# A gated one-hot made by ScalarE from an absolute difference and a relu, in a one-core decoder layer

## The chip, the cores and the metric

The kernel runs on one core of a Trainium2 chip. The metric is the device time of one execution in microseconds (us). TensorE (PE) multiplies matrices into PSUM, VectorE (DVE) and ScalarE (ACT) work element by element, GpSimd (POOL) here only issues gathers, and SyncE (SP) issues the other transfers. Each engine works through its own list of instructions in order and waits for others by semaphores.

## What is computed

One layer of a decoder trunk for a prompt of 1024 tokens (8 tiles of 128) and 8 single-token samples. After the mixers (attention, spatial gating, a recurrent block) comes a layer of product-key experts. Cut to what matters:

```python
s = einsum('nhpe,hpke->nhpk', q, sub_keys)           # 8 heads, two key sets of 128
v1, i1 = top_k(s[:, :, 0], 16); v2, i2 = top_k(s[:, :, 1], 16)
sv, ci = top_k(all sums of v1 and v2, 16)             # 16 experts a head
e_idx = i1[...] * 128 + i2[...]                       # one of 16384 experts
g = softmax(sv)
act = gelu(einsum('nd,nkd->nk', x, u_tab[e_idx]))     # 128 experts a token
out = einsum('nk,nkd->nd', g * act, v_tab[e_idx])
```

Each token has 128 chosen experts, each with a first index i1, a second index i2 and a gate g, all in float32.

## The kernel before

The expert layer is done in two ways. Four tiles of tokens (0, 2, 6, 7) and the sample are **gathered**: for each of 128 slots GpSimd fetches the 128 rows of the table that the tile's tokens chose (an indirect DMA, line 916, five buffers named grow), VectorE multiplies and sums them against the tokens (line 924, table u) or adds them, scaled, to acc (lines 931 and 933, table v). That is 520 fetches from each table, in the order tile 0, 2, 6, 7, sample, u before v in each tile.

The four other tiles (1, 3, 4, 5) are **dense**: all 16384 experts are applied. For this a gate table is built, for each token a matrix of 128 by 128 with the gate at (i2, i1) and zero elsewhere. `select(t)` brings i1, i2 and g of a tile with tokens along the free side into `tr`. `gate_table(t)` walks through the tile in 8 steps of 16 tokens. For 4 tokens at a time VectorE makes one-hot rows of i1 and of i2 by comparing a row of 0..127 (`iof`) with the index (line 815, tile `oh12`); ScalarE scales the one-hot of i1 by the gate into `o1` (line 822, three buffers); TensorE multiplies the two one-hots (line 823, into the one bank psG), which sums over the 128 slots; ScalarE copies psG into two tiles `st` (line 825, two buffers in all), and SyncE writes these to DRAM (`g_d`). `dense()` then computes scores of all experts (line 1022), gelu, times the gate table (line 1027), splits into two parts for exact products (lines 991 and 992), and products with table v (line 1038) that stay in PSUM (psK) or are added to acc by VectorE (psO, line 1047), in 32 groups of 4 blocks of 128 experts.

The order of the program text is: four groups of tiles are projected and mixed (`project`, `mix_and_route`), the steps of `select` and `gate_table` of a dense tile are pumped into the attention and the routing of the next group, then `dense()`, then the gathers. A scheduler of the language orders each engine's list from this text by its own estimate of when things are ready, with earlier text first; the gathers, last in the text, fill gaps. So the row operations of lines 924, 931 and 933 stand spread over VectorE's whole list, from the second group on, and the list is fixed when the kernel is built. "The front" below is all up to the first split of `dense()` (line 992, x0l).

Of the kernel before, what the change touches and what calls it, by code (L numbers as in the profile page):

```python
# [10 lines left out]
F32 = mybir.dt.float32  # L11
# [49 lines left out]
def kernel(ctx: ExitStack, tc: tile.TileContext, I, O):  # L61
# [41 lines left out]
    class Early:  # L103
# [2 lines left out]

        def a2(self, name):
            self.n += 1
            shape, tag = (([P, P // 2, TB], "st"), ([P, 2, OHB, P], "oh12"))[self.n % 2]
            x = fr.tile(shape, F32, tag=tag, name=name, bufs=2)  # L110
            return x.rearrange("p a b -> p (a b)")[:, :512] if tag == "st" else x.rearrange("p a b c -> p (a b c)")[:, :512]
    X = Early()

    def a4(name):
# [656 lines left out]
    def select(t):  # L771
        if t == NT:

            tv[t] = (se.tile([P, 16, 16], F32, tag="tkv", name="tkv", bufs=3), se.tile([P, 16, 16], U32, tag="tki", name="tki", bufs=3))
            v1, x1 = (q[:, 0, :] for q in tv[t])
            sr = R.a2("sr")[:, :P]
            S.dma_start(sr, s_d.rearrange("b (s k) -> (b s) k", k=P))
            top16(sr, P, v1, x1, "tkw", P)
            S.dma_start(sv_d, v1)
            S.dma_start(sx_d, x1)  # L780
            v, x = (q[:64, 2:4, :] for q in tv[t])
            S.dma_start(v, sv_d.rearrange("(q two) k -> q two k", two=2))
            S.dma_start(x, sx_d.rearrange("(q two) k -> q two k", two=2))
            r, nh = 64, 1
        else:
            r, nh = P, 8
            v, x = tv[t]
        tv.pop(t)
        i1, i2, gt = (se.tile([P, 8, 16], F32, tag=nm, name=nm, bufs=1)[:r, :nh] for nm in ("d_i1", "d_i2", "d_g"))
        yield from select_experts(v, x, r, nh, i1, i2, gt)  # L790
        if t in h2_d:
            e = se.tile([P, 8, 16], I32, tag="d_q4", name="d_e", bufs=1)[:r, :nh]
            V.scalar_tensor_tensor(e, i1, float(P), i2, op0=ALU.mult, op1=ALU.add)
            for d, src in ((e_d[t], e), (w_d[t], gt)):
                S.dma_start(dram_ap(d, 0, [[16 * nh, r], [1, 16 * nh]]), src.rearrange("p h k -> p (h k)"))
            return
        ps = R.ps("psi")
        tr[t] = fr.tile([P, 3, P], F32, tag="tr", name="tr", bufs=2)
        for q, src in enumerate((i1, i2, gt)):
            T.transpose(ps[:, q * P:(q + 1) * P], src.rearrange("p h k -> p (h k)"), ident)  # L800
        A.copy(tr[t], ps[:, :3 * P].rearrange("p (q n) -> p q n", q=3))

    def gate_ps(name):
        return mm.tile([P, 512], F32, tag="pg", name=name, bufs=BANKS["g"])
# [1 line left out]
    def gate_table(t):  # L806
# [3 lines left out]
        for b in range(P // TB):  # L810
            sts = [fr.tile([P, P // 2, TB], F32, tag="st", name="st", bufs=2) for _ in range(2)]
            for n0 in range(0, TB, 4):
                if n0 % OHB == 0:
                    oh = fr.tile([P, 2, OHB, P], F32, tag="oh12", name="oh12", bufs=2)
                    V.tensor_tensor(oh, iof[:, None, None, :].to_broadcast([P, 2, OHB, P]),  # L815
                                    tt[:, 0:2, b * TB + n0:b * TB + n0 + OHB, None].to_broadcast([P, 2, OHB, P]),
                                    op=ALU.is_equal)
                ps = gate_ps("psG")
                for q in range(4):
                    n = b * TB + n0 + q  # L820
                    o1 = fr.tile([P, P], F32, tag="o1", name="o1", bufs=3)
                    A.activation(o1, oh[:, 0, n0 % OHB + q, :], AF.Copy, scale=tt[:, 2, n:n + 1])  # L822
                    T.matmul(ps[:, q * P:(q + 1) * P], oh[:, 1, n0 % OHB + q, :], o1, start=True, stop=True)  # L823
                for st, pv in zip(sts, ps.rearrange("p (n two c) -> two p c n", n=4, two=2)):
                    A.copy(st[:, :, n0:n0 + 4], pv)  # L825
            hg = P // GST // 2
# [376 lines left out]
```

## Time and profile before

| | |
|---|---|
| median of 3 runs | 3299.31 us (3297.56 to 3300.51) |
| profiled execution | 3299.12 us, span 3297.3 us |
| PE busy | 2775.9 us, 84% of the span |
| DVE busy | 2543.4 us, 77% |
| ACT busy | 1213.0 us, 37% |
| POOL busy | 1412.7 us, 43% |
| transfers | 952.64 MB, mean 289 GB/s |

Busy shares are means over the whole span, and the program has parts with different limits: read a share by the stretch. A matmul's busy time is modelled and overlaps its neighbours. The idle time of an engine tells what ended it, which is not always what the program waits for last.

### The profile page before, as it was taken

To read this page: it belongs to the slowest core of one execution; us is meant where nothing else is said; L and a number is where in the kernel's file an instruction comes from. 1 tells how busy PE (TensorE), PEld (TensorE's weight loads), DVE (VectorE), ACT (ScalarE), POOL (GpSimd) and SP (SyncE) were. 2 spreads that over 40 slices of the span, in tenths; PEclk is the share of its full clock that TensorE was granted. 3 is DMA by queue.
4 is the path that set the end of the run, shared out by engine and by line. 5 is a ranking of instruction groups with operands and counts; after the bars stand their busy time and mean duration, and the time that the engine had idled before them with its cause. 6 is when DMAs were issued, how large, how long until landed. Compare 5 with 4: busy or idle time off the path is not lost.

```text
span 3297.3 us, 35948 instructions
## 1 busy us (share of the span) xinstructions
PE 2775.9 (84%) x11152; PEld 1877.4 (57%) x11152; DVE 2543.4 (77%) x5342; ACT 1213.0 (37%) x2718; POOL 1412.7 (43%) x1046
## 2 busy tenths in 40 slices
PE   6889877888898799768699989988998989989980
PEld 2334435443365346544477877766777777767760
DVE  1432776788777797777998898788988888889895
ACT  3454336553476337654432222221322222222210
POOL 0000033454234322334146666465656646666564
PEclk8989988989899899878899999999999999999995
DMA  7555487988778876888789999899999999999986
GB/s 250 179 191 198 142 287 227 311 317 297 238 224 287 314 252 195 266 281 284 239 297 349 352 321 334 322 341 335 337 331 338 343 332 357 330 344 346 342 299 226
DMA packets 340719, 952.64 MB, mean 289 GB/s; under 512 B 35600, under 2 KB 118087, under 8 KB 338479
## 3 DMA queue, kind: packets, MB, share of 16 engines
q0 software_dynamic: 149760, 545.33, 47.0%
q1 hardware_dynamic: 190766, 405.02, 35.1%
q8 instruction: 88, 1.44, 0.2%
q14 instruction: 105, 0.85, 0.1%
HBM read 894.07 MB, written 60.88 MB: 290 GB/s over the span
## 4 chain that ended last, share of the span: by engine, by line
PE 26%; DMA 23%; issue 21%; POOL 16%; DVE 10%; ACT 4%; SPq 0%; POOLq 0%; DVEq 0%; ACTq 0%
POOL grow L916 16%; PE psz L249 10%; DMA grow<-in_peer_v,ge 9%; DMA g_d<-st 5%; PE psG L823 4%; PE pst L174 2%; PE pso L637 2%; PE lg L620 2%; DMA w<-in_w_in 1%; DVE grow L924 1%; PE psa L206 1%; DVE acc L933 1%; DMA grow<-in_peer_u,ge 1%; DMA w<-in_wq 1%; PE psS L1022 1%
## 5 line engine op out<-in xcount | busy, mean ns | idle before, releaser
L916 POOL DMA_INDIRECT grow<-in_peer_u,ge x520 | 699.2, 1345 | 1146.8 <-DVE grow L924 466.5
L916 POOL DMA_INDIRECT grow<-in_peer_v,ge x520 | 712.9, 1371 | 717.1 <-DVE acc L933 420.9
L933 DVE SCALAR_TENSOR_TENSOR acc<-grow,dot,acc 128x1024 f32<-128x1024 f32 x515 | 659.8, 1281 | 121.8 <-DMA grow<-in_peer_v,ge 115.0
L249 PE MATMUL psz<-w,hT 128*128 128x512 f32 x1408 | 699.3, 629 | 61.7 <-DMA w<-in_w_in 22.4
L924 DVE SCALAR_TENSOR_TENSOR grow<-grow,gx 128x1024 f32<-128x1024 f32 x520 | 626.1, 1219 | 152.9 <-DMA grow<-in_peer_u,ge 120.0
L249 PEld LDWEIGHTS psz<-w,hT 128*128 128x128 f32 x1408 | 257.6, 200 | 325.8 <-issue 228.3
L1038 PE MATMUL psO<-vh,ah 128*128 128x512 f32 x512 | 223.6, 437 | 139.3 <-DVE acc L1047 138.8
L991 ACT CAST vh<-v 128x1024 fp32r<-128x1024 f32 x128 | 125.2, 1048 | 495.1 <-PE psO L1038 493.2
L823 PEld LDWEIGHTS psG<-o,oh 128*128 128x128 f32 x1024 | 162.5, 220 | 168.3 <-ACT st L825 106.7
L823 PE MATMUL psG<-o,oh 128*128 128x128 f32 x1024 | 195.0, 323 | 74.9 <-ACT st L825 70.0
L991 ACT CAST ah<-a 128x512 fp32r<-128x512 f32 x128 | 79.7, 622 | 424.1 <-DVE a L1027 424.1
L815 DVE TENSOR_TENSOR oh<-iof,tr 128x1024 f32<-128x1024 f32 x128 | 156.4, 1224 | 94.8 <-PE psG L823 92.8
L1038 PE MATMUL psO<-vl,ah 128*128 128x512 f32 x512 | 217.5, 425 | 0.0
L1038 PE MATMUL psO<-vh,al 128*128 128x512 f32 x512 | 215.5, 421 | 0.0
L991 ACT CAST uh<-u 128x1024 fp32r<-128x1024 f32 x128 | 135.0, 1055 | 218.4 <-PE psS L1022 218.0
L1038 PEld LDWEIGHTS psO<-vh,ah 128*128 128x128 f32 x512 | 107.7, 210 | 178.0 <-DVE acc L1047 154.2
L822 ACT ACTIVATE o<-oh,tr 128x128 f32<-128x128 f32 x512 | 185.0, 400 | 50.9 <-PE psG L823 46.5
L1038 PE MATMUL psK<-vh,ah 128*128 128x512 f32 x512 | 200.0, 391 | 2.1 <-ACT ah L991 2.1
L1038 PE MATMUL psK<-vh,al 128*128 128x512 f32 x512 | 200.2, 391 | 0.2 <-DVE al L992 0.2
L1038 PE MATMUL psK<-vl,ah 128*128 128x512 f32 x512 | 199.9, 390 | 0.0
L992 DVE TENSOR_TENSOR ul<-u,uh 128x1024 fp32r<-128x1024 f32 x128 | 156.0, 1219 | 1.4 <-ACT uh L991 1.4
L992 DVE TENSOR_TENSOR vl<-v,vh 128x1024 fp32r<-128x1024 f32 x128 | 150.5, 1219 | 0.5 <-ACT vh L991 0.4
(370 smaller groups left out, 5009.1 us busy)
## 6 DMA issues: line engine op xcount, KB each, us to landing
u<-in_peer_uT SPq DMA_DIRECT2D x128, 512.0 KB
v<-in_peer_v SPq DMA_DIRECT2D x128, 512.0 KB
w<-in_w_in SPq DMA_DIRECT2D x80, 512.0 KB
w<-in_wq SPq DMA_DIRECT2D x64, 512.0 KB
g_d<-st SPq DMA_DIRECT2D x64, 512.0 KB
gc<-g_d SPq DMA_DIRECT2D x16, 2048.0 KB
w<-in_w_ada SPq DMA_DIRECT2D x48, 512.0 KB
w<-in_w_out SPq DMA_DIRECT2D x32, 512.0 KB
```

What stands on the lines that cost most here:

```text
L174: T.transpose(pv[:, c, :r], src[:, (c0 + c) * P:(c0 + c + 1) * P], ident[:r, :r])
L249: T.matmul(ps, xT[:, c, :], w(c), start=(c == 0), stop=(c == 7))
L620: T.matmul(l[:, :k1 - k0], qT[t][64 * hh:64 * hh + 64, hp, :], kT[64 * hh:64 * hh + 64, k0:k1], start=True, stop=True)
L815: V.tensor_tensor(oh, iof[:, None, None, :].to_broadcast([P, 2, OHB, P]), tt[:, 0:2, b * TB + n0:b * TB + n0 + OHB, None].to_broadcast([P, ...
L822: A.activation(o1, oh[:, 0, n0 % OHB + q, :], AF.Copy, scale=tt[:, 2, n:n + 1])
L823: T.matmul(ps[:, q * P:(q + 1) * P], oh[:, 1, n0 % OHB + q, :], o1, start=True, stop=True)
L916: G.indirect_dma_start(out=rt, out_offset=None, in_=tab, in_offset=bass.IndirectOffsetOnAxis(ap=idx, axis=0))
L924: V.scalar_tensor_tensor(rt, rt, 1.0, x, op0=ALU.mult, op1=ALU.mult, accum_out=w[:, k:k + 1])
L933: V.scalar_tensor_tensor(acc, rt, w[:, k:k + 1], acc, op0=ALU.mult, op1=ALU.add)
L991: A.copy(hi, x)
L992: eng.tensor_tensor(lo, x, hi, op=ALU.subtract)
L1038: T.matmul(ps, aa[x][:, t * P:(t + 1) * P], vv[y][:, hf * 512:(hf + 1) * 512], start=(k == 0 and (first or o not in keep)), stop=(k == 3 * ...
```

## The change

The one-hot of i1 with its gate is no longer a comparison on VectorE followed by a scaling on ScalarE. ScalarE makes it in two passes from the row 0..127: first |i1 - c| with the index as the bias column, then relu(g - g|i1 - c|), with the gate as the bias column and the negated gate as the scale column. Where c is the index this is g, elsewhere the argument is zero or below and the result zero. VectorE's comparison makes the one-hot of i2 alone. `tr` has a fourth part for the negated gates, and the one-hot tile is half as large with three buffers in place of two; the early sample attention, which borrows these tiles, alternates over the new ones.

```diff
 def a2(self, name):   # Early
-            shape, tag = (([P, P // 2, TB], "st"), ([P, 2, OHB, P], "oh12"))[self.n % 2]
-            x = fr.tile(shape, F32, tag=tag, name=name, bufs=2)
+            shape, tag = (([P, P // 2, TB], "st"), ([P, OHB, P], "oh2"))[self.n % 2]
+            x = fr.tile(shape, F32, tag=tag, name=name, bufs=2 if tag == "st" else 3)
...
-        tr[t] = fr.tile([P, 3, P], F32, tag="tr", name="tr", bufs=2)
+        tr[t] = fr.tile([P, 4, P], F32, tag="tr", name="tr", bufs=2)
...
-        A.copy(tr[t], ps[:, :3 * P].rearrange("p (q n) -> p q n", q=3))
+        A.copy(tr[t][:, 0:3, :], ps[:, :3 * P].rearrange("p (q n) -> p q n", q=3))
+        A.activation(tr[t][:, 3, :], tr[t][:, 2, :], AF.Copy, scale=-1.0)
...
-                    oh = fr.tile([P, 2, OHB, P], F32, tag="oh12", name="oh12", bufs=2)
-                    V.tensor_tensor(oh, iof[:, None, None, :].to_broadcast([P, 2, OHB, P]),
-                                    tt[:, 0:2, b * TB + n0:b * TB + n0 + OHB, None].to_broadcast([P, 2, OHB, P]),
+                    oh = fr.tile([P, OHB, P], F32, tag="oh2", name="oh2", bufs=3)
+                    V.tensor_tensor(oh, iof[:, None, :].to_broadcast([P, OHB, P]),
+                                    tt[:, 1, b * TB + n0:b * TB + n0 + OHB, None].to_broadcast([P, OHB, P]),
                                     op=ALU.is_equal)
...
-                    A.activation(o1, oh[:, 0, n0 % OHB + q, :], AF.Copy, scale=tt[:, 2, n:n + 1])
-                    T.matmul(ps[:, q * P:(q + 1) * P], oh[:, 1, n0 % OHB + q, :], o1, start=True, stop=True)
+                    A.activation(o1, iof, AF.Abs, bias=tt[:, 0, n:n + 1], scale=-1.0)
+                    A.activation(o1, o1, AF.Relu, bias=tt[:, 2, n:n + 1], scale=tt[:, 3, n:n + 1])
+                    T.matmul(ps[:, q * P:(q + 1) * P], oh[:, n0 % OHB + q, :], o1, start=True, stop=True)
```

Since the scheduler orders every engine's list anew, far more rows change place than the diff has lines. Lines after 800 are numbered up to three higher in the kernel after: 815 is 816, 822 is 824 and 825, 825 is 828, 924 is 927, 933 is 936, 1047 is 1050, 1066 is 1069 and 1067 is 1070.

ScalarE, at the start of the last gate table (tile 5): the copy to `tr`, then the first one-hots. Before, with copies and an exponential of the attention between them:

```order
L801 COPY tr<-psi 128x384
L822 ACTIVATE o_8911<-oh_8908,tr 128x128
L825 COPY st<-psG 128x64x4 x2
L822 ACTIVATE o_8914<-oh_8908,tr 128x128
L822 ACTIVATE o_8917<-oh_8908,tr 128x128
L822 ACTIVATE o_8920<-oh_8908,tr 128x128
L635 COPY pT<-pst 128x512 x2
```

The same place now:

```order
L801 COPY tr<-psi 128x384
L802 ACTIVATE tr<-tr 128x128
L824 ACTIVATE o_9859<-iof,tr 128x128
L824 ACTIVATE o_9863<-iof,tr 128x128
L825 ACTIVATE o_9859<-o_9859,tr 128x128
L825 ACTIVATE o_9863<-o_9863,tr 128x128
L824 ACTIVATE o_9867<-iof,tr 128x128
```

One instruction for a token has become two, and two tokens are taken in turns; the negation stands behind the copy.

VectorE, at the last addition to x1 of the fourth group (line 714, tiles 6 and 7), with the row operations of tile 2 around it. Before:

```order
L815 TENSOR_TENSOR oh_9612<-iof,tr 128x1024
L924 SCALAR_TENSOR_TENSOR grow,dot<-grow,gx 128x1024
L815 TENSOR_TENSOR oh_9629<-iof,tr 128x1024
L712 TENSOR_TENSOR tmp<-psz,g1r 128x512
L815 TENSOR_TENSOR oh_9646<-iof,tr 128x1024
L714 TENSOR_TENSOR x_10046<-x_10046,tmp 128x512
L156 TENSOR_SCALAR nv<-ssq 128x1
```

The same place now:

```order
L712 TENSOR_TENSOR tmp<-psz,g1r 128x512
L936 SCALAR_TENSOR_TENSOR acc<-grow,dot,acc 128x1024
L714 TENSOR_TENSOR x_10528<-x_10528,tmp 128x512
L936 SCALAR_TENSOR_TENSOR acc<-grow,dot,acc 128x1024 x4
L712 TENSOR_TENSOR tmp<-psz,g1r 128x512
L936 SCALAR_TENSOR_TENSOR acc<-grow,dot,acc 128x1024
L714 TENSOR_TENSOR x_10530<-x_10530,tmp 128x512
```

Tile 2 stood in its pass over table u here; now that pass is done and it stands in its pass over table v, and the last one-hots lie ahead of this place.

VectorE, the end of the list. Before, from the last evacuation of psO (line 1047) on:

```order
L1047 TENSOR_TENSOR acc_10913<-acc_10913,psO 128x512
L1066 TENSOR_TENSOR tmp<-grw,acc_10912 128x512
L1066 TENSOR_TENSOR tmp<-grw,acc_10913 128x512
L933 SCALAR_TENSOR_TENSOR acc<-grow,dot,acc 128x1024
L1067 TENSOR_TENSOR x1f<-x1f,tmp 128x1024
L933 SCALAR_TENSOR_TENSOR acc<-grow,dot,acc 128x1024 x19
L940 TENSOR_TENSOR acc<-acc,grw 128x1024
L941 TENSOR_TENSOR acc<-acc,x1f 128x1024
L924 SCALAR_TENSOR_TENSOR grow,dot<-grow,gx 128x1024 x8
```

The same place now:

```order
L1069 TENSOR_TENSOR tmp<-grw,acc_11427 128x512
L1070 TENSOR_TENSOR x1f<-x1f,tmp 128x1024
L1050 TENSOR_TENSOR acc_11428<-acc_11428,psO 128x512
L1069 TENSOR_TENSOR tmp<-grw,acc_11428 128x512
L1050 TENSOR_TENSOR acc_11429<-acc_11429,psO 128x512
L1069 TENSOR_TENSOR tmp<-grw,acc_11429 128x512
L1070 TENSOR_TENSOR x1f<-x1f,tmp 128x1024
```

The row operations that stood behind the dense part, those of tile 7 and of the sample, are gone from here; the list ends with the dense part's own output.

## Rows read from the trace of the kernel before

**Rows 1.** The page: the gathers' queue (packets, MB, share), then groups: count | busy us, mean ns | idle.
```profile
q0 software_dynamic: 149760, 545.33, 47.0%
...
L916 POOL DMA_INDIRECT grow<-in_peer_u,ge x520 | 699.2, 1345 | 1146.8 <-DVE grow L924 466.5
...
L933 DVE SCALAR_TENSOR_TENSOR acc<-grow,dot,acc 128x1024 f32<-128x1024 f32 x515 | 659.8, 1281 | 121.8 <-DMA grow<-in_peer_v,ge 115.0
...
L924 DVE SCALAR_TENSOR_TENSOR grow<-grow,gx 128x1024 f32<-128x1024 f32 x520 | 626.1, 1219 | 152.9 <-DMA grow<-in_peer_u,ge 120.0
...
L815 DVE TENSOR_TENSOR oh<-iof,tr 128x1024 f32<-128x1024 f32 x128 | 156.4, 1224 | 94.8 <-PE psG L823 92.8
...
L822 ACT ACTIVATE o<-oh,tr 128x128 f32<-128x128 f32 x512 | 185.0, 400 | 50.9 <-PE psG L823 46.5
```

**Rows 2.** Stretches: length, busy PE, PEld, DVE, ACT, POOL, then PEclk, DMA share, GB/s.
```profile
496.00:657.00 161.00, 132.94 (x580) 81.36 (x580) 112.19 (x196) 100.08 (x294) 64.77 (x49) 0.86 0.80 266
657.00:894.00 237.00, 200.94 (x647) 87.26 (x647) 195.10 (x810) 100.64 (x275) 96.22 (x72) 0.92 0.84 296
894.00:1074.00 180.00, 157.20 (x731) 99.06 (x730) 135.36 (x216) 124.24 (x343) 68.04 (x50) 0.91 0.75 246
1074.00:1236.00 162.00, 138.48 (x413) 67.87 (x414) 138.01 (x565) 61.48 (x162) 53.04 (x42) 0.91 0.80 282
1236.00:1527.00 291.00, 230.29 (x1109) 156.00 (x1108) 214.36 (x396) 185.53 (x538) 97.60 (x72) 0.85 0.75 249
1527.00:1592.00 65.00, 44.95 (x152) 22.55 (x150) 59.57 (x288) 19.33 (x70) 26.30 (x22) 0.86 0.78 272
1592.00:3205.00 1613.00, 1454.45 (x6144) 1185.40 (x6144) 1404.67 (x1850) 420.24 (x537) 934.75 (x681) 0.94 0.92 332
```

**Rows 3.** Groups by line, the longer list: count | busy us, mean ns | idle.
```profile
L1027 DVE TENSOR_TENSOR a<-a,gc 128x512 f32<-128x512 f32 x128 | 87.8, 686 | 6.0 <-DMA gc<-g_d 5.0 <-ACT a L1025 1.0
...
L924 DVE DVE_READ_ACCUMULATOR grow<-grow,gx 128x1 f32 x520 | 42.2, 81 | 0.0
...
L341 ACT ACTIVATE hT<-pst,modT_sh,modT_sc 128x128 f32<-128x128 f32 x96 | 38.1, 459 | 29.3 <-DVE hT L339 29.3
```

**Rows 4.** Waits from 1236 to 1527 us: total us, times, longest.
```profile
PEld psG L823 <- ACT st L825: 67.8, 41, 10.3
...
ACT st L825 <- DMA g_d<-st: 46.0, 19, 9.8
ACT o L822 <- PE psG L823: 26.2, 42, 3.8
```

**Rows 5.** The chain of waits at the front's end: start us, us, what.
```profile
1518.05 5.30 DMA g_d<-st
...
1533.72 11.29 DMA w<-in_wq
...
1588.86 3.32 DMA xr<-xT_d
```

**Rows 6.** Lines 992, 1047, 1067: ns min/median/max, first and last start.
```profile
L992 DVE TENSOR_TENSOR x0l<-xr,x0h x1: 692/692/692, 1592.2 to 1592.2; 128x512 fp32r<-128x512 f32 x1
...
L1047 DVE TENSOR_TENSOR acc<-acc,psO x124: 674/681/689, 1704.4 to 3204.6; 128x512 f32<-128x512 f32 x124
...
L1067 DVE TENSOR_TENSOR x1f<-x1f,tmp x4: 1218/1218/1219, 3189.6 to 3207.6; 128x1024 f32<-128x1024 f32 x4
```

**Rows 7.** The chain of waits at the program's end: start us, us, what.
```profile
3244.49 4.60 DMA out_xp<-acc
3249.10 8.47 DMA gx<-h_d
```

**Rows 8.** The front's busiest 100 us by transfers, columns as in rows 2.
```profile
600.00:700.00 100.00, 81.67 (x312) 42.26 (x312) 79.33 (x170) 54.85 (x133) 55.51 (x42) 0.93 0.96 343
```

**Rows 9.** The page: the first matmul of a group into psO.
```profile
L1038 PE MATMUL psO<-vh,ah 128*128 128x512 f32 x512 | 223.6, 437 | 139.3 <-DVE acc L1047 138.8
```

More of the change, by code (lines that the diff above doesn't have):

```diff
@@ L108, in a2 @@
             self.n += 1
-            shape, tag = (([P, P // 2, TB], "st"), ([P, 2, OHB, P], "oh12"))[self.n % 2]
-            x = fr.tile(shape, F32, tag=tag, name=name, bufs=2)
-            return x.rearrange("p a b -> p (a b)")[:, :512] if tag == "st" else x.rearrange("p a b c -> p (a b c)")[:, :512]
+            shape, tag = (([P, P // 2, TB], "st"), ([P, OHB, P], "oh2"))[self.n % 2]
+            x = fr.tile(shape, F32, tag=tag, name=name, bufs=2 if tag == "st" else 3)
+            return x.rearrange("p a b -> p (a b)")[:, :512]
     X = Early()
```

## Prediction

> **What bounds the kernel now.** I read the page first (its busy shares, its slices, its costliest groups), then a table of busy time by stretch, then the waits inside the stretch with most gate-table work, then the chain at the end of the front and at the end of the program. The profiled execution took 3299.1 us with a span of 3297.3 us, so 1.8 us lie around the span; the median of the runs is 3299.3 us, 0.2 us away. The sum below is made against 3299.1.
>
> The program has a front (routing, attention, gate tables) up to the first dense split on VectorE at 1592.2 us, a dense part up to the last evacuation of psO at 3204.6 us, and a tail of 93 us [rows 6]. Beside both run 1040 row operations, 520 of L924 and 520 of L931 and L933: GpSimd fetches 128 rows of 4 KB, VectorE consumes the block [rows 1]. 545.33 MB by 1040 is 0.524 MB for one [rows 1]. They stand at fixed places in VectorE's order, so VectorE can neither run ahead of them nor leave one for later.
>
> The dense part is full: TensorE 1454 of 1613 us busy, VectorE 1405, and the transfer engines at a share of 0.92 with 332 GB/s [rows 2]. The tail is the last row operations, the sample's eight rows and their small transfers, one after another [rows 7]. In the front no engine is full over a whole stretch [rows 2]. Where gate tables are built, the waits go in a ring: the weight load of psG waits for the copy to st, that copy waits for the write of st to DRAM, and the scaled one-hot waits for psG to give back its o tile [rows 4]. The end of the front is reached through that write, then through the loads of w_q and of xr [rows 5].
>
> **The change part by part.** *VectorE* makes 4 one-hots in one instruction in place of 4 pairs: 128 instructions of 128x1024 elements at 1224 ns [rows 1] become 128 of 128x512, priced by the product of that size at 686 ns [rows 3]. That takes 128 x 0.54 = 69 us off VectorE, all in the front. *ScalarE* keeps one pass over 128x128 (Abs for Copy, 400 ns [rows 1]) and gains 512 Relu with a column as scale and a column as bias. The nearest row has both columns too: L341 with 459 ns [rows 3]; the row of L822, with one column, gives 400 ns and is the lower bound. So 512 x 0.46 = 236 us more (205 by the lower bound). The four negations of the gates (128x128, a row in the ACT order below) and the four column-wider tr tiles are under 2 us together. ScalarE is busy 100.1 of 161 us, 124.2 of 180 and 185.5 of 291 in the three table stretches [rows 2]; with 59, 59 and 118 us more it would fill 159 of 161, 183 of 180 and 304 of 291. So the stretches get longer if nothing else does it.
>
> The Trainium skill, page "ScalarE: Activation LUTs", section "Rules for kernel authors", speaks against this move: relu, add and multiply belong on VectorE. By that page's figures (186 ns, 93 ns for each column operand, 0.833 ns an element) one Relu would be an estimated 479 ns and the addition 245 us; the row's 459 ns agrees within 5%, and the sum goes by the row.
>
> *The order* moves much more than these two. Where ScalarE has more to do, row operations fill VectorE's order. I marked the stretches of rows 2 by the same VectorE instruction in both orders (the first one-hot of the first table, the first convolution tap of the third projection, and so on) and counted row operations between them. 496 to 657 us: 47 before, 106 now. 657 to 894: 71 and 55. 894 to 1074: 50 and 101. 1074 to 1236: 41 and 37. 1236 to the first dense split: 93 and 189. In all 323 stand ahead of the first dense split before, 507 now; after the last evacuation stand 36 before and none now. The transfers that feed them come earlier with them: GpSimd's queue keeps its order, and a fetch starts when VectorE gives a buffer back.
>
> *Price in the front.* In each stretch I add the bytes of the added operations to those moved there (rate by length) and divide by 332 GB/s, what the engines moved over the dense part with the same mix of streams [rows 2].
> - 496 to 657: 161 x 0.266 = 42.8 MB, plus 59 x 0.524 = 30.9, is 73.7 MB or 222 us: +61.
> - 894 to 1074: 44.3 + 26.7 = 71.0 MB or 214 us: +34.
> - 1236 to 1592: 72.5 + 17.7 + 50.3 = 140.5 MB or 423 us for 356: +67.
> - The other two stretches lose 20 operations of 1.30 us (L924 with its accumulator read, or L933 [rows 1, 3]), 26 us of VectorE at 0.82 and 0.85 busy [rows 2]; I take half: -13.
>
> Sum +149 us. VectorE alone asks for less: in 1236 to 1592, 214.4 + 59.6 + 96 x 1.30 - 35 = 364 us for 356. The transfers set the price, ScalarE stands close behind, and the wait for st gets worse, since those writes go through the same engines. Bounds: if the bytes spread evenly over 496 to 1592 us, 293 + 186 x 0.524 = 391 MB at 332 GB/s take 1177 us for 1096, +81; at the 343 GB/s of the front's busiest 100 us [rows 8] they take 1139, +43. From above, all of ScalarE's 236 us on the path and nothing hidden. I take +149 because the operations are bunched in the three table stretches and an in-order VectorE can't spread them.
>
> *Price behind the front.* The dense part keeps its pace while row operations last: between the 1st and the 89th L1047 stand 479 before and 489 now. Then three things are saved. Between the first split and the first L1047 5 operations fewer: -6. The last row operation now stands at the 97th of 124 L1047, so nearly seven groups of four run without any. TensorE waits 138.8 us in 32 groups for VectorE's evacuation [rows 9], 4.3 us a group; seven would give 29, and I take two thirds, -20, since VectorE has splits of its own there. The tail: before, 92.7 us from the last L1047 to the end; now two products, one sum (to 3208.8 us on the old scale [rows 6]) and one output write of some 5 us remain [rows 7], 9 us: -84. Together -110.
>
> **Sum:** 3299.1 + 149 - 110 = 3338 us, 1.2% slower. The point at which it turns is +110 in the front.
>
> **The rivals.** *Faster: the front absorbs the row operations.* The orders fix places, not times; the front's idle transfer time (shares of 0.75 and 0.80 in the table stretches [rows 2]) may take the bytes more evenly than my three stretches say, because transfers run up to five buffers ahead. Then the front costs +81 or, at 343 GB/s, +43, and the result is 3270 or 3232 us. For it: the tail is surely empty of row operations, and VectorE has 77 us idle of 291 in the longest table stretch. Against: TensorE and ScalarE follow VectorE's order, and every block that comes late now holds up an evacuation of the front. Chance 0.29.
>
> The Trainium skill, page "Perfetto Trace Analysis", section "Roofline", puts a single core's ceiling at about 435 GB/s of its 16 transfer engines; by that figure the 391 MB would be an estimated 898 us, under the 1096, and transfers would not lengthen the front at all. No row here stands near it: the busiest 100 us of the front show 343 GB/s at a share of 0.96 [rows 8].
>
> *Slower still: ScalarE becomes the bound.* The Relu stands between the Abs and the matmul, and psG has one bank: if the ring of waits [rows 4] lets none of it run beside the write of st, the 236 us all lie on the path, and 3299 + 236 - 110 = 3425 us. Against: ScalarE waits 46 us for st and 26 us for psG in the longest stretch [rows 4], which can take some of it. Chance 0.10.
>
> *No change: both halves cancel.* At a front longer by 103 to 117 us the time stays within 0.2%, about what a measurement of this kernel can tell from no change. It needs about two thirds of the forecast's lengthening. Chance 0.11.
>
> *The back isn't won.* If the seven groups without row operations go no faster, 20 us of the 110 are lost and the result is 3358 us; this lies within the forecast.
>
> **How the numbers follow.** Forecast 3338 us, chance 0.50, with a range of its own from 3307 to 3380. With ScalarE's rival slower has 0.60; faster 0.29; same 0.11. The range of 8 in 10 reaches from 3240, almost all of the faster rival, to 3405, short of ScalarE's whole price.
>
> **What would show it.** Right: the first L992 starts near 1741 us, 149 later; the share of the transfer engines in the stretches of tables is 0.9 or more; L924 and L933 wait longer for blocks there; the last L1047 is followed by some 9 us; the one-hots take about 0.69 us and the Relu about 0.46. Wrong: the first L992 before 1700 us (then the front absorbed it, and the time is below 3299); ScalarE over 90% busy in the table stretches, with VectorE and the transfers waiting for it (then ScalarE is the bound); a dense part shorter by more than 50 us (then row operations cost it more than I say); row operations still behind the last evacuation.

## The result, and the profile after

The kernel after takes 3557.59 us (median of 6 runs, 3535.85 to 3564.88), the kernel before 3291.18 in the same comparison: ratio 1.0809, 95% interval 1.0783 to 1.0836. That is 8.1% slower, where 3338 us was forecast with a range to 3405. The sign was right, the size far off.

The profiled execution took 3564.88 us with a span of 3563.1. Single instructions of the first dense split, of the evacuation of psO, and the end of the chain of waits of the kernel after (duration in ns min/median/max, first and last start in us; in the chain start, us, what):

```profile
L995 DVE TENSOR_TENSOR x0l<-xr,x0h x1: 693/693/693, 1968.9 to 1968.9; 128x512 fp32r<-128x512 f32 x1
...
L1050 DVE TENSOR_TENSOR acc<-acc,psO x124: 674/682/690, 2086.4 to 3556.7; 128x512 f32<-128x512 f32 x124
...
3556.67 0.70 DVE acc L1050
...
3557.39 0.70 DVE tmp L1069
...
3558.12 1.23 DVE x1f L1070
```

Against [rows 6] the front is longer by 377 us (1592.2 to 1968.9; +149 was forecast), and the rest is shorter by 111 (3297.3 - 1592.2 = 1705.1, now 1594.2; -110 was forecast). So the error of the sum is in the front. The changed operations alone cost about what the prediction says. The page of the kernel after, groups by line (count | busy us, mean ns | idle before):

```profile
L825 ACT ACTIVATE o<-o,tr 128x128 f32<-128x128 f32 x512 | 228.7, 486 | 0.2
...
L824 ACT ACTIVATE o<-iof,tr 128x128 f32<-128x128 f32 x512 | 195.7, 396 | 53.6 <-PE psG L826 52.5
...
L816 DVE TENSOR_TENSOR oh<-iof,tr 128x512 f32<-128x512 f32 x128 | 87.7, 691 | 173.4 <-PE psG L826 171.6
```

Next I cut the front at the first and last one-hots of each gate table. Busy time by stretch, the four tables and the stretch between the first two, kernel before and then after (length, busy PE, PEld, DVE, ACT, POOL with counts, PEclk, DMA share, GB/s):

```profile
496.00:638.00 142.00, 116.18 (x514) 74.04 (x514) 99.46 (x174) 90.33 (x273) 53.56 (x41) 0.84 0.78 255
638.00:910.00 272.00, 233.11 (x774) 103.99 (x773) 219.13 (x864) 120.54 (x315) 110.22 (x82) 0.91 0.81 287
910.00:1049.00 139.00, 118.57 (x603) 78.70 (x602) 102.66 (x154) 105.09 (x304) 48.37 (x35) 0.93 0.77 249
...
1251.00:1381.00 130.00, 109.73 (x591) 76.82 (x587) 98.60 (x161) 96.29 (x276) 31.84 (x24) 0.89 0.67 211
1384.00:1527.00 143.00, 102.79 (x419) 67.82 (x419) 101.79 (x202) 80.20 (x243) 56.18 (x43) 0.79 0.82 282
```

```profile
504.00:673.00 169.00, 94.32 (x342) 68.66 (x340) 101.25 (x177) 112.73 (x325) 86.26 (x65) 0.56 0.76 260
673.00:1000.00 327.00, 282.99 (x943) 128.42 (x943) 252.08 (x895) 145.51 (x388) 124.33 (x98) 0.89 0.79 278
1000.00:1169.00 169.00, 112.45 (x389) 75.83 (x388) 113.62 (x137) 118.58 (x337) 89.11 (x68) 0.59 0.79 259
...
1451.00:1619.00 168.00, 107.75 (x398) 71.45 (x394) 96.29 (x179) 116.83 (x331) 72.08 (x54) 0.65 0.71 241
1654.00:1822.00 168.00, 89.37 (x332) 63.56 (x332) 107.45 (x116) 112.54 (x319) 87.70 (x66) 0.60 0.74 252
```

Two things stand there that the prediction doesn't have. In the tables nothing is full: in the first, ScalarE is busy 113 of 169 us, and the transfers stand at 0.71 to 0.79 in all four. And TensorE has fewer records in a table than before (342 for 514, 389 for 603), more between the tables (943 for 774). A record isn't yet a product: the 512 float32 products into psG leave 1024 records in each kernel. Which work left the first table is read from TensorE's groups by line inside it, before and after:

```profile
L823 PE MATMUL psG<-o,oh 128*128 128x128 f32 x240 | 46.6, 329 | 10.8 <-ACT st L825 8.7 <-ACT o L822 2.0
L249 PE MATMUL psz<-w,hT 128*128 128x512 f32 x70 | 38.1, 651 | 4.5 <-ACT hT L341 3.1 <-DMA w<-in_w_out 1.4
L637 PE MATMUL pso<-pT,vt 128*64 128x128 f32 x84 | 15.7, 330 | 4.4 <-DMA vt<-vt_d 4.4
```

```profile
L826 PE MATMUL psG<-o,oh 128*128 128x128 f32 x232 | 67.0, 437 | 43.4 <-ACT o L825 24.9 <-ACT st L828 18.5
L637 PE MATMUL pso<-pT,vt 128*64 128x128 f32 x62 | 14.5, 396 | 22.5 <-ACT pT L635 19.3 <-DMA vt<-vt_d 3.2
...
L249 PE MATMUL psz<-w,hT 128*128 128x512 f32 x2 | 1.1, 637 | 0.0
```

The projections and part of the attention that ran beside the table have been ordered behind it: 70 records of psz became 2 in the table, and 283 became 350 between the first two tables. In TensorE's lists, 749 products and transposes other than psG stood inside the four tables before (174, 235, 232 and 108), and 380 after (76, 110, 120 and 74). TensorE waits longer in a table with less other work (43.4 us of idle time before psG in the first, 10.8 in the kernel before), and the work that was its cover takes time of its own later.

### The profile page after: what moved, and what is told of

Same layout as the page of the kernel before. It is cut to its first block, busy times and chain, and to the rows that moved or that the text cites. A ratio compares the mean times of both kernels' runs of the same rounds, so it can differ in the third digit from the quotient of the medians.

```text
span 3563.1 us, 36414 instructions
## 1 busy us (share of the span) xinstructions
PE 2913.9 (82%) x11152; PEld 1959.2 (55%) x11152; DVE 2486.0 (70%) x5342; ACT 1413.2 (40%) x3229; POOL 1393.5 (39%) x1046
## 4 chain that ended last, share of the span: by engine, by line
PE 35%; DMA 23%; issue 15%; POOL 11%; DVE 8%; ACT 7%; SPq 0%; POOLq 0%; DVEq 0%; ACTq 0%
POOL grow L919 11%; PE psz L249 10%; DMA g_d<-st 8%; DMA grow<-in_peer_v,ge 6%; PE psS L1025 5%; PE psG L826 5%; PE psO L1041 4%; PE pso L637 2%; PE psK L1041 2%; PE pst L174 2%; ACT o L825 2%; DVE acc L936 2%; ACT st L828 2%; PE lg L620 2%; ACT o L824 1%
## 5 line engine op out<-in xcount | busy, mean ns | idle before, releaser
L919 POOL DMA_INDIRECT grow<-in_peer_v,ge x520 | 700.5, 1347 | 687.8 <-DVE acc L936 352.5
L249 PE MATMUL psz<-w,hT 128*128 128x512 f32 x1408 | 690.4, 628 | 50.9 <-DMA w<-in_w_in 17.2
L826 PE MATMUL psG<-o,oh 128*128 128x128 f32 x1024 | 285.9, 419 | 209.0 <-ACT st L828 114.2
L826 PEld LDWEIGHTS psG<-o,oh 128*128 128x128 f32 x1024 | 215.6, 284 | 316.3 <-ACT o L825 149.2
L825 ACT ACTIVATE o<-o,tr 128x128 f32<-128x128 f32 x512 | 228.7, 486 | 0.2
L824 ACT ACTIVATE o<-iof,tr 128x128 f32<-128x128 f32 x512 | 195.7, 396 | 53.6 <-PE psG L826 52.5
L816 DVE TENSOR_TENSOR oh<-iof,tr 128x512 f32<-128x512 f32 x128 | 87.7, 691 | 173.4 <-PE psG L826 171.6
```

The lines of the kernel that those rows point to most:

```text
L249: T.matmul(ps, xT[:, c, :], w(c), start=(c == 0), stop=(c == 7))
L816: V.tensor_tensor(oh, iof[:, None, :].to_broadcast([P, OHB, P]), tt[:, 1, b * TB + n0:b * TB + n0 + OHB, None].to_broadcast([P, OHB, P]), ...
L824: A.activation(o1, iof, AF.Abs, bias=tt[:, 0, n:n + 1], scale=-1.0)
L825: A.activation(o1, o1, AF.Relu, bias=tt[:, 2, n:n + 1], scale=tt[:, 3, n:n + 1])
L826: T.matmul(ps[:, q * P:(q + 1) * P], oh[:, n0 % OHB + q, :], o1, start=True, stop=True)
L919: G.indirect_dma_start(out=rt, out_offset=None, in_=tab, in_offset=bass.IndirectOffsetOnAxis(ap=idx, axis=0))
```

## The experiments

"Front" below is the start of the first dense split in the profiled execution. "Row operations" are those in VectorE's list ahead of it. The kernel before ran beside each group, with medians between 3283 and 3291 us; a run given without a ratio was executed once. Where a kernel is built anew, the scheduler orders every list anew; this turned out to matter as much as the edits, and the last group holds the lists for this reason.

### Is it the second pass?

e1 leaves the Relu out of the kernel after (the gate tables are then not the reference's); e2 adds a Relu with scale 1 and bias 0 to the kernel before, whose o1 it doesn't change.

```diff
-                    A.activation(o1, o1, AF.Relu, bias=tt[:, 2, n:n + 1], scale=tt[:, 3, n:n + 1])
```
```diff
                     A.activation(o1, oh[:, 0, n0 % OHB + q, :], AF.Copy, scale=tt[:, 2, n:n + 1])
+                    A.activation(o1, o1, AF.Relu, bias=zo[:, 0:1], scale=zo[:, 1:2])
```

> The kernel after with the Relu left out: ScalarE makes one pass (Abs) for a token, as before, VectorE the half comparison; o1 holds |i1 - c| and no gate, so the gate tables hold other numbers. 376 row operations stand ahead of the first dense split (before 323, after 507). Theory 'ring' (the second pass on ScalarE lengthens the cycle Abs, Relu, matmul, copy to st, write): the front ends at 1592 us or earlier, time 3230 to 3300. Theory 'row operations' (each one moved into the front costs it about 2 us, 377 us by 184): 53 more cost +109 in the front and give back some 30 behind it, time about 3380.

> The kernel before with a second pass of ScalarE over o1 (a Relu with a column of zeros as bias and a column of ones as scale, which changes nothing in o1): the second pass alone, with VectorE's full comparison and the old tiles. 491 row operations stand ahead of the first dense split. 'Ring': the front ends at 1900 to 2000 us, time 3500 to 3600, as after, since the pass is the cause. If VectorE's smaller one-hot or the new tiles had a part in the loss, the time stays under 3450.

e1: 3276.9 us, front 1652, 376 row operations. e2: 3512.9 us, front 1917, 491. So a second ScalarE pass, whatever it computes, brings most of the loss, as the theory 'ring' says, and without it the change is near the time of before, though its front ends 60 us later than that theory allows. This doesn't yet say how, since either run is in a new order, and the order goes over with the pass: between the first and the last record of psG of the four tables TensorE has 1152 other records in the kernel before and 1200 in e1, but 524 in e2 and 594 in the kernel after. e2 has VectorE's full comparison and the old tiles, so these aren't what turns the order.

### Is it the row operations?

e3 is the kernel before without the gathered tiles and the sample's experts, e4 the kernel after without them. e5 is the kernel after with the gathers of tiles 2, 6 and 7 behind the first dense split, and the sample's behind those.

```diff
-    for t in GATHER:
-        peer_prompt(t)
-    peer_sample()
```

> The kernel before without the gathered tiles' expert layer (no row operations, no gathers, four tiles and the sample get no output). Gives the front's end without row operations, first dense split. 'Row operations': it falls well below 1592 us, by 323 x 1.3 = 420 us of VectorE's time at most, to 1200 to 1400. 'Ring': the tables and attention keep it above 1400.

> The kernel after without the gathered tiles' expert layer. To be held against e3_before_no_rows, the first dense split. 'Row operations' (the 184 more in the front are what costs 377 us): its front ends less than 130 us after that of e3_before_no_rows. 'Ring' (with the order of the lists that follows from it): 250 us after or more. The stretches of tables then also show whether the write of st still takes 12 us from issue, and whether TensorE's granted clock still stands near 0.5 of full speed without gathers.

> The kernel after with the row operations of tiles 2, 6 and 7 queued behind the first dense split on VectorE: 256 stand in the front (after 507). 'Ring' (ScalarE's second pass in the table's cycle, 307 of the front's 377 us without any row operation): the front ends only 40 to 110 us earlier than after's 1969, at 1860 to 1930, the back gets longer, the whole stays at 3530 to 3640. 'Row operations': the front falls below 1750.

e3: 2803.3 us, front 1383; e4: 3108.6, front 1690. Without any row operation the front still grows, by 307 us. e5: 3638.9 us, front 1828 with 251 row operations fewer, but the rest 1809, 215 longer. With 256 row operations, fewer than the 323 of before, the front is still 236 us longer than before. So moved row operations can't be the main cause, and taking them out of the front here cost more behind it than it won.

### Is it the order?

e10 is e4 with TensorE's list up to the dense part held in the order of e3; e11 is e3 with TensorE's list in the order of e4. The order is held by dependencies between neighbours in the list that wait for nothing. The other engines' lists are the scheduler's. Both leave the gathered tiles out, like e3 and e4.

```diff
+    for u, v in zip(want, want[1:]):
+        tc.add_manual_dep(pe[v], pe[u].name, mybir.DependencyInfo(mybir.DependencyClass.NoSync, mybir.DependencyReason.DATA), reason="order")
```

> e4_after_no_rows (after, no row operations; its front ends at 1690 us, that of e3_before_no_rows at 1383) with TensorE's list in the front held, instruction by instruction, to the order it has in e3_before_no_rows; the other engines are ordered anew around it. Theory 'order' (the table's steps stand ahead of the attention in TensorE's list, so that the mixing and routing no longer run beside the tables): the front ends at 1383 to 1500 us. Theory 'pass' (ScalarE's second pass makes each step longer wherever it stands): 1640 us or later.

> The other way round: e3_before_no_rows with TensorE's list in the front held to the order it has in e4_after_no_rows. 'Order': the front ends at 1550 us or later with ScalarE's work of before. 'Pass': it stays under 1450.

e10: 3006.4 us, front 1587, that is 203 more than e3 and 104 fewer than e4. e11: 3026.3, front 1606, 223 more than e3 with the same work. So the new order of TensorE's list costs by itself, about as much as the pass in the old one, and the two don't add up to the 307 us of e4. Neither theory of e10 held: its front lies between their ranges. e11 is as 'order' says.

### Is it TensorE's clock?

The granted clock in the four tables fell from 0.79 to 0.93 before to 0.56 to 0.65 after (above), that is, close to the lower of its two levels, 1.2 GHz in place of 2.4, and the median of a psG record rose from 276 to 421 ns. From 550 to 650 us, before and then after, in two pieces of 50 us (the table of the kernel before ends at 638):

```profile
550.00:600.00 50.00, 40.93 (x176) 26.73 (x174) 34.80 (x65) 35.37 (x105) 17.38 (x13) 0.79 0.73 233
600.00:650.00 50.00, 44.55 (x196) 22.73 (x196) 41.25 (x69) 25.69 (x76) 27.68 (x20) 1.00 0.96 330
```

```profile
550.00:600.00 50.00, 24.38 (x86) 18.31 (x85) 25.74 (x46) 28.64 (x82) 22.66 (x19) 0.50 0.75 258
600.00:650.00 50.00, 27.36 (x93) 20.52 (x93) 30.41 (x52) 34.94 (x100) 25.30 (x20) 0.50 0.75 257
```

TensorE is busy for half of the stretch there, at exactly half of the clock. The Trainium skill, page "TensorE: Matmul & The Clock Gate", section "What's actually happening", knows these two levels and no others; 0.50 and 1.00 agree.

e8 issues each product into psG twice, in the kernel after. e13 is e4 with the first three of four products issued three times; the fourth, for which the copy to st waits, stays single. e14, e15 and e17 do the same as e13 to the kernel after, the kernel before and e4, and hold all five engines' lists in the order that each has without the added products.

```diff
-                    T.matmul(ps[:, q * P:(q + 1) * P], oh[:, n0 % OHB + q, :], o1, start=True, stop=True)
+                    for _ in range(3 if q < 3 else 1):
+                        T.matmul(ps[:, q * P:(q + 1) * P], oh[:, n0 % OHB + q, :], o1, start=True, stop=True)
```

> The kernel after with each matmul into psG issued twice (the second writes the same again): TensorE's work in the tables doubled, nothing else. Theory 'clock' (TensorE idles in the table stretches, its granted clock falls to 0.5, and all its work there takes longer, which is most of the loss): the granted clock in the stretches rises from 0.65 to 0.85 or more and the front ends earlier than 1969. 'Ring' alone: the clock may rise, but the last matmul of four still waits for the last Relu, and the front ends at 1969 or up to 100 us later.

> e4_after_no_rows with the first three matmuls of each four into psG issued three times (six more for four tokens, the last one, which the copy to st waits for, only once): TensorE is kept busy while ScalarE works on the next tokens. Theory 'clock': the granted clock in the table stretches rises from 0.62 to 0.74 to 0.9 or more, and the front ends 60 us or more before 1690. If the low clock is only a mark of TensorE's waiting, the front ends at 1680 or later.

> The kernel after, all five engines' lists held in its own order, and the first three of every four products into psG issued three times in a row (the fourth, which the copy to st waits for, once). Theory A: a good part of the 377 us is the granted TensorE clock, which stands at 0.50 to 0.67 in its table stretches; the added products keep TensorE busy, the clock rises to 0.9 or more, the front shortens by 60 to 130 us and the time is about 3430 to 3500. Rival B: the ring of Abs, Relu, product, copy and write sets the stretches and the clock only shows that TensorE waits; then the added products bring nothing or cost a few us, and the time is 3550 to 3580.

> The kernel before with the same added products, all lists held in its own order. Its table stretches stand at a clock of 0.85 to 0.91, so A has less to give back: 20 to 50 us less, 3240 to 3270. B: 3287 to 3300.

> The kernel after without gathered tiles, with the same added products, all lists held in the order that it has without them (3108.6 us). The run with these products in lists that the scheduler had ordered anew gave 2985.4. If the clock did that (A), this gives some 2985 to 3010 too; if the new order did it (B), it stays at 3100 to 3115. The four gathered tiles and the sample's experts are left out.

| | mean clock without | with | front without | with | time |
|---|---|---|---|---|---|
| e8, new order | 0.858 | 0.898 | 1969 | 1997 | 3575.2 |
| e13, new order | 0.905 | 0.977 | 1690 | 1565 | 2985.4 |
| e17, order of e4 | 0.905 | 0.962 | 1690 | 1740 | 3159.9 |
| e14, order of after | 0.858 | 0.914 | 1969 | 2009 | 3621.3, ratio 1.1017 (1.0970 to 1.1063) |
| e15, order of before | 0.906 | 0.922 | 1592 | 1690 | 3394.2, ratio 1.0307 (1.0259 to 1.0354) |

e13 misled me: alone it reads as 125 us given back by the clock. But its four tables take 564 us where those of e4 take 551; what it won lies between and behind them (519 for 654 us), where the other work stands. With the lists held (e17) the same instructions at nearly the same clock cost 50 us instead. e13 and e17 execute the same work and differ by 174 us, by their order. In all three held kernels the clock rose and the front became longer, by more than either theory of e14 allowed. In the tables of e14 the clock stands at 0.82 to 0.89, and the median of a psG record is back at 276 ns, but the tables take 739 us for 674. The added products of three tokens stand in TensorE's list ahead of the product that the copy to st waits for, so they are not off the ring as I had meant; that the clock gives back nothing at all is therefore not shown, only that it is worth less than these products cost. The Trainium skill, the same page, section "HAM oscillation — how this bites in real kernels", advises to restructure or pad work so that TensorE stays at full clock. Read as advice to add products, it would make e14 gain; the mean clock rose from 0.858 to 0.914, and the front became 40 us longer.

### Buffers, another engine, other places

e9 gives o1 five buffers. e7 lets VectorE make the gated one-hot in one instruction (is_equal, then mult) and ScalarE none; e12 is e7 with its row operations put early by ordering dependencies, 486 in the front.

```diff
-                    A.activation(o1, iof, AF.Abs, bias=tt[:, 0, n:n + 1], scale=-1.0)
-                    A.activation(o1, o1, AF.Relu, bias=tt[:, 2, n:n + 1], scale=tt[:, 3, n:n + 1])
+                    V.tensor_scalar(o1, iof, tt[:, 0, n:n + 1], tt[:, 2, n:n + 1], op0=ALU.is_equal, op1=ALU.mult)
```

> The kernel after with five o1 buffers for three. If ScalarE loses time because the o1 tiles come back late (52 us of waits for psG's matmuls before its Abs, and no work ahead while the write of st is awaited), the front ends 50 us or more earlier than 1969. If the two passes themselves, or the order of the lists, make the loss, it moves by less than 30 us.

> The kernel after with both passes of ScalarE replaced by one instruction of VectorE for a token (compare iof with the index column, times the gate column, 128x128), ScalarE makes no one-hot at all. 256 row operations ahead of the first dense split. 'Ring': ScalarE's share of the cycle goes from 0.86 us a token to none, the front ends at 1592 or earlier, time 3150 to 3300. If VectorE is the engine that can't take more (0.2 to 0.4 us a token more than the half comparison, 100 to 200 us in the front), the front ends after 1592 and the time is above 3300.

> e7_vector_onehot (3321 us: its front ends at 1510, but only 256 row operations stand in it, and the part behind takes 1805 us) with row operations pinned evenly into VectorE's list of the front, 486 of them ahead of the first dense split. If a row operation costs the front 0.4 to 0.6 us (e4 and e5 against after) and saves about 0.9 us behind it (e5 against after), 230 of them cost 90 to 140 and save some 200: 3220 to 3280 us, faster than before. If VectorE is full there (it would be busy for about 1400 of 1510 us), the front grows by 230 x 1.3 = 300 us and the time is above 3400.

e9: 3540.1 us, front 1959, so the buffers of o1 weren't what held it. The wait for an o tile falls from 52.5 to 7.5 us, but that of the copy for the write of st stays at 154.5 us (154.3 in the kernel after), and TensorE's weight loads of psG wait 217.9 us for copies to st, for 133.9 in the kernel after. Its lists are new too: 279 instructions of other work stand in TensorE's four tables, for 380. The time comes out 0.5% below the kernel after. e7: 3321.4 us, ratio 1.0110 (1.0075 to 1.0146); its front, 1510, is the shortest of the kernels with all their work, with 256 row operations, and the rest is longer by 100. e12: 3489.0 us, ratio 1.0597 (1.0543 to 1.0650), front 1918: early row operations by force are not cheap either. e7 and e12 move VectorE's load and the lists together, so neither prices a single cause.

### The parts one by one, in held lists

e18 is the change itself with all five lists in the order of the kernel before: each Relu right behind its Abs, the negation behind its copy, all else in its old place. e20 is e18 but with the gathered tiles' own instructions free, so that the scheduler places row operations anew (512 in the front, none behind the last psO, against 507 and none in the kernel after). e19 is the kernel after in its own order on all engines, without the Relu (its gate tables are not the reference's).

```diff
-                    A.activation(o1, o1, AF.Relu, bias=tt[:, 2, n:n + 1], scale=tt[:, 3, n:n + 1])
+                    A.activation(o1, o1, AF.Relu, bias=tt[:, 2, n:n + 1], scale=tt[:, 3, n:n + 1], again=A.last)
...
+    for n in array.array("H", zlib.decompress(base64.b64decode(ORDER))):
+        if n == 65535:
+            for u, v in zip(want, want[1:]):
+                tc.add_manual_dep(v, u.name, mybir.DependencyInfo(mybir.DependencyClass.NoSync, mybir.DependencyReason.DATA), reason="order")
```

> The change itself, with every engine's list held in the order of the kernel before (each Relu right behind its Abs, each negation behind its copy, all else as before). No row operation moves, none is won at the end. Theory C (the second pass lies in the ring of the table): the front grows by about what it grew without row operations when TensorE's old order was held, 203 us, so the first dense split starts near 1795 and the time is about 3495. Theory of the prediction (the front grows because row operations are moved into it): nearly nothing is left of the growth, under 40 us, and the time is 3290 to 3330. All of ScalarE's passes on the path: 512 x 0.486 = 249 us, 3536.

> The change, all lists held in the order of before except the gathered tiles' own instructions, which the scheduler places anew: 512 row operations now stand ahead of the first dense split in place of 323, and none behind the last psO, nearly as in the kernel after. Against the run with all held (3404, front 1692, back 1708) this prices the prediction's own step. By its bytes the front grows by 149 to 1841 and the back falls to 1594: 3437. By the 0.4 us for one that the kernels without row operations point to, the front is 1768 and the time 3364. If the idle transfer time takes them, the front stays at 1692 and the time is 3290. If row operations in new places are what undoes the front, 1969 and 3560 return.

> The kernel after in its own order on all five engines, without the Relu (the gate tables are not the reference's). With the change in the order of before (front 1692) and the kernel after (1969) this makes the third corner. Theory D: the new order itself carries most of the 277 us between them; then the front stays near 1850 and the time near 3440. Theory E: the new order only costs because the second pass stands in it; then the front falls to 1690 or less, and the time to 3250 to 3290, about that of the run without the Relu in an order of its own (front 1652, 3277).

e18: 3404.2 us, ratio 1.0351 (1.0305 to 1.0398). e20: 3410.4, ratio 1.0375 (1.0332 to 1.0418). e19: 3484.6, ratio 1.0592 (1.0557 to 1.0627). The first dense splits of e18, e20 and e19 (all VectorE calls go through one wrapper there, line 77):

```profile
L77 DVE TENSOR_TENSOR x0l<-xr,x0h x1: 691/691/691, 1692.0 to 1692.0; 128x512 fp32r<-128x512 f32 x1
```

```profile
L77 DVE TENSOR_TENSOR x0l<-xr,x0h x1: 693/693/693, 1833.7 to 1833.7; 128x512 fp32r<-128x512 f32 x1
```

```profile
L77 DVE TENSOR_TENSOR x0l<-xr,x0h x1: 693/693/693, 1894.6 to 1894.6; 128x512 fp32r<-128x512 f32 x1
```

No run holds a kernel's lists and changes nothing else, so what the holding itself costs is not measured. But e18 agrees with the kernel before within 6 us in each part outside the tables. The front in parts, from the starts of the first and the last one-hot of each table in the traces ("to the split" is what follows the last table), with row operations inside the tables, and the rest of the span:

| | before the tables | four tables | between them | to the split | front | row operations in tables | rest |
|---|---|---|---|---|---|---|---|
| before | 496 | 553 | 478 | 65 | 1592 | 140 | 1705 |
| e18: pass | 491 | 655 | 475 | 71 | 1692 | 140 | 1708 |
| e20: pass, row operations | 493 | 794 | 485 | 62 | 1834 | 339 | 1575 |
| after: all | 504 | 674 | 644 | 147 | 1969 | 253 | 1594 |
| e19: new order, no Relu | 507 | 620 | 624 | 144 | 1895 | 253 | 1589 |

From row to row: the pass in unchanged order costs 100 us in the front, all of it in the tables. The row operations' new places cost 142 more, 138 of it in the tables, and win 133 behind the front. The last 135 are what the order of everything else costs, taken as the difference: the tables are 119 us shorter, since work and row operations left them, and the stretches between and behind them 243 longer, with 11 ahead of them. 100 + 142 + 135 = 377. This is one way through the differences, and the parts depend on it: the row operations were priced with 339 in the tables, and the kernel after has 253 there. None of the theories of e18 held: 100 us lie between the 40 of the prediction's and the 203 of the pass. e20 is near 'by its bytes' (1834 for 1841). e19 is as theory D says, and stronger.

What each of the first two does is seen in the tables. Their stretches in e18 and then in e20, columns as above:

```profile
491.00:653.00 162.00, 122.73 (x502) 74.13 (x502) 82.71 (x174) 141.64 (x388) 48.27 (x41) 0.83 0.71 228
...
924.00:1096.00 172.00, 138.49 (x606) 82.70 (x602) 86.98 (x156) 161.07 (x426) 42.51 (x35) 0.90 0.62 203
...
1296.00:1461.00 165.00, 126.05 (x585) 84.18 (x583) 80.95 (x159) 149.49 (x393) 29.48 (x23) 0.82 0.53 165
1464.00:1621.00 157.00, 112.54 (x413) 64.87 (x412) 84.87 (x200) 133.79 (x362) 50.48 (x43) 0.85 0.75 254
```

```profile
493.00:693.00 200.00, 128.05 (x502) 77.73 (x502) 142.19 (x274) 142.13 (x386) 110.50 (x90) 0.79 0.89 311
...
963.00:1160.00 197.00, 144.59 (x590) 88.27 (x590) 154.91 (x239) 158.86 (x418) 111.86 (x91) 0.83 0.91 325
...
1370.00:1571.00 201.00, 139.82 (x579) 93.79 (x575) 153.14 (x250) 153.14 (x394) 105.59 (x86) 0.72 0.83 287
1577.00:1772.00 195.00, 120.27 (x413) 70.56 (x412) 130.58 (x191) 134.78 (x361) 83.91 (x68) 0.75 0.81 283
```

ScalarE's waits for the write of st over the whole run, in e18 and then in e20 (us in total, times, longest; 81.4 us in the kernel before, 154.3 after):

```profile
ACT st L77 <- DMA g_d<-st: 19.7, 13, 3.9
```

```profile
ACT st L77 <- DMA g_d<-st: 142.1, 49, 7.8
```

In e18 TensorE has its old cover, but ScalarE is busy 161 of 172 us in the second table and 0.85 to 0.91 of the others: with the old neighbours in the tables, ScalarE is the bound, or close to it. Over the four tables it has 214 us more to do than before (586 for 372), and 102 us of that lengthen them; the rest went into time in which it had waited, the waits for the write of st above all (81.4 to 19.7 us). The clock (0.90 in the second table, 0.93 before, with a mean of 0.906 in both runs) can have little part in this. In e20 these waits come back, 122 us more than in e18, with the transfers at 0.81 to 0.91. So the row operations lengthen the ring of waits mainly through the write of st. The pages' chains of the work that ended last say the same: ScalarE has 4% of the span on it before, 16% in e18 and 9% in e20, the writes of st 5%, 2% and 8%. In the kernel after, the second table has ScalarE at 119 of 169 us and transfers at 0.79.

e19 comes from the other side: in the new order, with its places of the row operations, the front without the Relu is still 302 us longer than before, and the Relu adds only 74 there. Most of the loss stays when the pass goes and its order stays. That the scheduler chose this order on account of the longer ScalarE work is what e1 and e2 point to; which estimate of it is wrong wasn't tried. How much of the order's price the low clock in its tables carries (0.56 to 0.65) isn't shown either.

## Why the prediction failed

**The back: right in sum.** -111 us for -110. The tail was right, -86 for -84 (92.7 to 6.4). Two smaller terms were off and cancelled by luck: from the split to the first psO +5 for the forecast -6 (112.2 to 117.5 us), the 124 evacuations -30 for -20 (1500.2 to 1470.3).

**The row operations' price in the front: the right cause, the right size partly by luck.** +149 was forecast, and e20 against e18 shows +142. The cause that the prediction names is there: "the wait for st gets worse" (19.7 to 142.1 us). But its rule, bytes at 332 GB/s, doesn't give this size where it was measured. With the bytes of e18's four tables and the operations that e20 adds there (51, 55, 62 and 31) it gives +77 us, for a measured +138, and the last two tables moved 287 and 283 GB/s. What the operations cost at the places that they have in the kernel after isn't shown. With -133 behind the front the two halves nearly cancel, +8 for the forecast +39.

**The Relu: slightly low as a price, wrong in its place.** 486 ns for the 459 of the nearest row [rows 3]. The Trainium skill's estimate, 479 ns from the figures of its page "ScalarE: Activation LUTs", section "What ACT_TABLE_LOAD costs", was the nearer one: the median is 480. The first step that failed is "The transfers set the price, ScalarE stands close behind": it put ScalarE's added time at nothing beside the transfers' price. It took the larger of two prices where the work stands in a ring. e18 shows 100 us for the pass alone, and e20 shows the row operations' 142 on top of it, not in its place: the pass had used up the waits in which the writes of st could have hidden. The hint was in the sum itself: 183 of 180 and 304 of 291 us of ScalarE means that stretches grow before a byte is added.

**The order: the second step that failed.** The prediction counted row operations between markers and took it that all other work stays between the same markers; its sum has no term for it. The lists of the two kernels show otherwise: TensorE has 749 instructions beside those of psG in the four tables before, 380 after. By the differences above this cost 135 us in the front. It is also where the stretches part from the forecast: the tables stand at transfer shares of 0.71 to 0.79, where 0.9 or more was to show the forecast right and e20, in the old order, has 0.81 to 0.91.

**The rivals.** The faster one had 0.29; the front didn't absorb the row operations, 142 us in e20 are more than its 43 or 81. "ScalarE becomes the bound", at 3425 us with 0.10, is near to what e18 shows in the tables, at 100 us rather than 236; the argument against it, that ScalarE's waits take some of the pass, was right. None had the other engines' order, so the range ended at 3405, and even "all of ScalarE's 236 us on the path" was no bound from above.

## What to carry to other kernels

Where a scheduler orders the lists, compare all of them around the change, above all how much other work stands inside a ring of waits that needs cover; a list that groups the ring's instructions together (380 others for 749 here) is a warning. Add the prices of engines that take turns in a ring rather than take the larger: each uses up the waits in which the other was to hide (100 and 142 us here). And when an experiment edits the program, hold the lists, or it measures the new order: the same instructions differed by 174 us here.

## What the runs showed of the hardware

TensorE's granted clock stood at 0.50 for 100 us at a stretch while it was half busy with small products between waits (24.4 and 27.4 of 50 us), and the median of a psG record rose from 276 to 421 ns. I took this for a main cause, and that isn't shown: raising the mean clock to 0.914 with extra products made the front 40 us longer, and the change in the old order lost 100 us at the old mean clock of 0.906. With 199 row operations more in the four tables, ScalarE's waits for the writes of st to DRAM rose from 19.7 to 142.1 us (e18 and e20).
